# Storing rotated queries and keys to DRAM with the part as the outer index

## The chip, the core and the metric

The kernel runs on one core of a Trainium2 chip. A core has TensorE (PE, matmuls; PEld is its weight load), VectorE (DVE), ScalarE (ACT), GpSimd (POOL) and SyncE (SP, which here only issues DMAs), and 16 DMA engines that move data between DRAM and the on-chip memory of 128 partitions. ACT issues some DMAs too. The metric is the device time of one execution in microseconds (us), as the median of several runs.

## What is computed

Two layers of a diffusion transformer over 1024 latent tokens of width 1024, with 256 context tokens as a prefix for the keys. The first layer puts a short gated convolution beside a differential attention with 2-D rotary positions; the second mixes by Fourier transforms. Each is followed by a squared-ReLU MLP. What matters here is the attention:

```python
def diff_attend(q, k, v, lam):
    s = jnp.einsum('bqhcd,bkhcd->bhcqk', q, k).astype(jnp.float32) * (DIFF_QK_DIM ** -0.5)
    p = jax.nn.softmax(s, axis=-1)
    pd = (p[:, :, 0] - lam * p[:, :, 1]).astype(v.dtype)
    return jnp.einsum('bhqk,bkhd->bqhd', pd, v)
...
            p = u @ w_in[j]
            q = rope_2d(heads_qk(p[..., Q0:K0]), row, col)
            k = rope_2d(heads_qk(p[..., K0:V0]), row, col)
            v = heads_v(p[..., V0:])
```

There are 4 heads (h), each with two halves (c) of 64 channels for q and k. A rotation takes pairs of channels, 32 pairs for a half.

## The kernel before

All matmuls are in float32 by splitting: an operand is a high part rounded to the short format plus a low rest, and a product is three matmuls (`mm3`, lines 89 to 91; `split`, line 98, makes the high part on ACT and the low part on another engine). The stages around the change run in this order:

- **Values** (to about 105 us): the normalized tokens are transposed into `UH`, `UL` (latent) and `CH`, `CL` (context), and v is projected.
- **Queries and keys** (about 105 to 230 us; line 540 on). For two pairs of heads (`hp`) and for q, then k (`which`), there are two weight tiles: tile `iA` gives the first channel of each rotated pair and `iA + 1` the second. A weight tile has 128 columns: (2 heads x 2 halves) x 32 pairs. PE multiplies tile `iA` with each block of 512 tokens (and for k with the 256 context tokens), then tile `iA + 1`; after each block of the second, `rotate` (line 431) makes four **parts** `rp0` to `rp3` on DVE, POOL and ACT: the two rotated channels, each as high and low part. A part is 128 rows x 512 tokens; its row index is (head, half) g = 0..3 times pair r = 0..31. The parts have three buffers each, so a block must be in DRAM before the third block after it is written.
- `rotate` returns four stores (line 448; line 560 for the context, which isn't rotated). `store` (line 379, its DMA is line 382) issues them on SP two blocks later.
- **Weights** come through ACT's own DMA queue: `w_load` (line 235, DMA on line 238) loads tile i + 2 into one of two `wraw`, and `w_parts` splits the next tile into `wh` on ACT and `wl` on POOL. ACT works in order: while a DMA that it is to issue has to wait, what stands behind waits too.
- Beside this, `Ada` loads slices `wa` of the modulation weights on SP (line 164, biases on line 186), seven ahead, and DVE sums them up (`tick`, lines 172 and 174).
- **Convolution** (about 230 to 375 us; line 574 on): twelve more weight tiles, two blocks each, with DVE work between, and its own stores `Ad` on line 382.
- **Attention** (375 to 600 us): for each head and half, `load_set(n)` (line 504) reads from DRAM a set with `q`, `k0`, `k1` and `kx` on 128 partitions, arranged as parts x pairs: `k0` is both high parts of k twice, `k1` and `kx` both low parts twice (latent and context tokens), and `q` its high and low parts in an order that depends on the half. There are eight sets in three buffers. Sets 0 to 2 are loaded before their use; sets 3, 5 and 7 take the buffer of a half that just finished and belong to the head that starts. `S` (lines 634 to 638) multiplies q with k, `M` takes the maximum (641), `E` the exponential on ACT (646).

The order of PE, DVE, ACT, POOL and SP is written out by hand up to the end of the convolution; after it, a scheduler orders the instructions by the due times in a table. Each engine, and SP's DMA queue, works in that order. All DMAs of SP and ACT share eight completion semaphores in turn, and one is issued only when the DMA before it on the same semaphore has landed.

The DRAM copies are `Qd` and `Kd`, one tensor for two heads each:

```python
    Qd = [dram.tile([4, 4, 32, N], F32, name=f"Qd{i}") for i in range(2)]
    Kd = [dram.tile([4, 4, 32, NK], F32, name=f"Kd{i}") for i in range(2)]
```

Before, their indices are (g, part, pair, token). A store of one part takes all four g, at a distance of four parts, and the 32 rows of each: 4 x 32 rows. A load takes two neighbouring parts of one g: 64 rows of one stride.

Of the kernel before, what the change touches and what calls it, by code (L numbers as in the profile page):

```python
# [21 lines left out]
N = 1024  # L22
NC = 256
D = 1024
KT = 8
NK = N + NC
# [7 lines left out]
def raw(ap):  # L34
    return ap.bitcast(F32)


def body(tc, nc, I, O, dbg=None):
# [10 lines left out]
    def popen(name, **kw):  # L49
        p = tc.alloc_tile_pool(name=name, bufs=kw.pop("bufs", 1), **kw)  # L50
        pools[name] = p
        return p

    def pclose(*names):
        for n in names:
            pools.pop(n).release()
# [41 lines left out]
    def split(hi, lo, src, eng=None):  # L98
        a = nc.scalar.copy(hi, src)  # L99
        return a, (eng or nc.vector).tensor_tensor(out=lo, in0=src, in1=raw(hi), op=ALU.subtract)  # L100
# [134 lines left out]
    def w_load(i):  # L235
        if i < len(wsrc):
            wraws[i] = pW.tile([P, D], F32, name="wraw", tag="wraw")
            nc.scalar.dma_start(out=wraws[i], in_=wsrc[i])
# [10 lines left out]
    def rows():  # L249
        return p0.tile([P, D], F32, name="xt", tag="xt", bufs=11)  # L250
# [48 lines left out]
    with tc.manual_schedule(engines={mybir.EngineType.PE, mybir.EngineType.DVE, mybir.EngineType.Activation,  # L299
# [3 lines left out]
        for k in range(KT):  # L303
            t = ([WVL, WVH] + UH + UL)[k % 6].rearrange("p k n -> p (k n)")
            for i in range(2):
# [4 lines left out]
                for j in range(2):  # L310
                    ps, c = aps[2 * i + j], slice(j * 512, j * 512 + 512)
# [67 lines left out]
    def store(*keep):  # L379
        while len(stores) > len(keep):  # L380
            for o, i in stores.pop(0):
                nc.sync.dma_start(out=o, in_=i)
# [33 lines left out]
    Qd = [dram.tile([4, 4, 32, N], F32, name=f"Qd{i}") for i in range(2)]  # L416
    Kd = [dram.tile([4, 4, 32, NK], F32, name=f"Kd{i}") for i in range(2)]
    Ad = [dram.tile([KT, P, N], F32, name=f"Ad{i}") for i in range(2)]
    def next_weights(i):
        w_load(i + 2)  # L420
        if i:
            w_parts(i + 1)

    def proj(i, bH, bL, n, tag="mm"):
        ps = ps1.tile([P, 512], F32, name="pj", tag=tag)
        wh, wl = wtiles[i]
        for k in range(KT):
            mm3(ps[:, :n], wh[:, k, :], wl[:, k, :], bH[:, k, :], bL[:, k, :], k == 0, k == KT - 1)
        return ps

    def rotate(pR, ada, pA, pB, c, dst, scale):
        parts = [pR.tile([P, 512], F32R, name=f"rp{i}", tag=f"rp{i}", bufs=3) for i in range(4)]
        t = [pR.tile([P, 512], F32, name=f"rt{i}", tag=f"rt{i}") for i in range(4)]
        nc.vector.tensor_tensor(out=t[0], in0=pA, in1=cosT[:, c], op=ALU.mult)
        nc.vector.tensor_tensor(out=t[2], in0=pB, in1=sinT[:, c], op=ALU.mult)
        nc.vector.tensor_tensor(out=t[1], in0=pA, in1=sinT[:, c], op=ALU.mult)
        nc.vector.tensor_tensor(out=t[3], in0=pB, in1=cosT[:, c], op=ALU.mult)
        nc.gpsimd.tensor_tensor(out=t[0], in0=t[0], in1=t[2], op=ALU.subtract)
        nc.gpsimd.tensor_tensor(out=t[1], in0=t[1], in1=t[3], op=ALU.add)
        ada.tick()  # L440
        for i in range(2):
            if scale is None:
                split(parts[i], parts[2 + i], t[i])
            else:
                nc.scalar.mul(parts[i], t[i], scale)
                nc.vector.scalar_tensor_tensor(out=parts[2 + i], in0=t[i], scalar=scale, in1=raw(parts[i]),
                                               op0=ALU.mult, op1=ALU.subtract)
        return [(dst[:, i, :, c], raw(parts[i])) for i in range(4)]


    class Conv:
# [52 lines left out]
    def load_set(n):  # L504
        h, c = n // 2, 1 - n % 2
        p = pools["pHqR" if n % 3 == 2 else "pHqL"]
        t = {nm: p.tile([P, w], F32R, name=nm, tag=f"{nm}{n % 3}")
             for nm, w in (("q", N), ("k0", NK), ("k1", N), ("kx", NC))}
        rows = lambda ap: ap.rearrange("i r n -> (i r) n")
        g = (h % 2) * 2 + c  # L510
        q, k = Qd[h // 2][g], Kd[h // 2][g]
        for i in range(2):
            r = slice(i * 64, i * 64 + 64)
            j = (i + c) % 2 * 2
            nc.sync.dma_start(out=raw(t["q"][r]), in_=rows(q[j:j + 2]))
            nc.sync.dma_start(out=raw(t["k0"][r]), in_=rows(k[0:2]))
            nc.sync.dma_start(out=raw(t["k1"][r]), in_=rows(k[2:4, :, 0:N]))
            nc.sync.dma_start(out=raw(t["kx"][r]), in_=rows(k[2:4, :, N:NK]))
        hsets[h, c] = t

    def load_v(h):
        vv = []
        for i in range(2):
            t = pHv.tile([P, 10, P], F32R, name=f"vs{i}", tag=f"vs{i}")
            nc.sync.dma_start(out=raw(t), in_=Vd[i][:, :, h * P:(h + 1) * P])
            vv.append(t)
        heads.setdefault(h, {})["v"] = vv
# [4 lines left out]
    with tc.manual_schedule(engines={mybir.EngineType.PE, mybir.EngineType.DVE, mybir.EngineType.Activation,  # L532
                                     mybir.EngineType.Pool, mybir.EngineType.SP}):
        w_load(2)
        cosT = pR.tile([P, N], F32, name="cosT", bufs=1)
        sinT = pR.tile([P, N], F32, name="sinT", bufs=1)
        nc.sync.dma_start(out=cosT, in_=I["rope_cos"])
        nc.sync.dma_start(out=sinT, in_=I["rope_sin"])
        ada = Ada(pAda, ada0[:4])
        for hp in range(2):  # L540
            for which in range(2):
                iA = hp * 4 + which * 2
                if iA:
                    next_weights(iA)
                blks = [(UH[b], UL[b], 512) for b in range(2)] + [(CH, CL, NC)] * which
                psA = []
                for blk in blks:
                    psA.append(proj(iA, *blk))
                    ada.tick(2)
                next_weights(iA + 1)  # L550
                dst = (Kd if which else Qd)[hp]
                for b, blk in enumerate(blks):
                    pB = proj(iA + 1, *blk, "tr")
                    if b < 2:
                        st = rotate(pR, ada, psA[b], pB, slice(b * 512, b * 512 + 512), dst, None if which else 0.125)
                    else:
                        parts = [pR.tile([P, 512], F32R, name=f"rp{i}", tag=f"rp{i}", bufs=3) for i in range(4)]
                        split(parts[0][:, :NC], parts[2][:, :NC], psA[b][:, :NC])
                        split(parts[1][:, :NC], parts[3][:, :NC], pB[:, :NC])
                        st = [(dst[:, i, :, N:NK], raw(parts[i][:, :NC])) for i in range(4)]  # L560
                    stores.append(st)
                    store(0, 1)
                    ada.tick()
        ada.tick(len(ada0) * KT)
        ada.end()
        store()
        pclose("pAda", "pR", "pUc")
        pC = popen("pC", bufs=1, side="right", **tile_waits)
        cb = [pC.tile([P, 514], F32, name=f"cb{i}") for i in range(2)]
        for b in range(2):  # L570
            nc.gpsimd.memset(cb[b][:, 0:1], 0.0)
        ada = Ada(popen("pAda", side="right", **tile_waits), ada0[4:])
        pHv = None
        for c in range(12):
            i = 8 + c
            cv = Conv(c)
            next_weights(i)
            for b in range(2):
                cv.Y(b)
            for b in range(2):  # L580
                ps = proj(i, UH[b], UL[b], 512, ("mm", "tr")[b])
                ada.tick(2)
                cv.V(b, ps)
                cv.O(b)
                if not b:
                    store()
            if c == 7:
                ada.tick(len(ada0) * KT)
            if c == 8:
                ada.end()  # L590
                pclose("pAda")
                popen("pHqL", side="left", **tile_waits)
                pHv = popen("pHv", bufs=2, side="left", **tile_waits)
                load_set(0)
            if c == 9:
                load_v(0)
                load_set(1)
        store()
# [246 lines left out]
    tiles.update({i: Tile(i) for i in range(32)})  # L845
    last = {c: PIPE["S", c, 1] for c in range(2)}
    at(-1.0, lambda: load_set(2))
    for n in range(3, 8):
        m = n - 3
# [4 lines left out]
    for h in range(4):  # L854
        k = PIPE["SC",] + 4 * h + 3
# [1138 lines left out]
```

## Time and profile before

| | |
|---|---|
| median of 3 runs | 2353.55 us (2352.23 to 2354.19) |
| the profiled execution | 2347.32 us, its span 2345.2 us |
| PE busy | 2130.1 us, 91% of the span, 9618 matmuls |
| DVE, ACT, POOL busy | 63%, 36%, 51% |
| granted TensorE clock, mean | 0.965 of full speed |
| the chain that ended last, by engine | PE 50%, DVE 16%, POOL 9%, DMA 9%, issue 6%, ACT 5%, SP's queue 2% |

The profile is one execution, and its rows are in its own time. An engine's busy share is an average over stages that have different limits; the waits of one stretch say who was late there. "SPq" and "ACTq" are the DMA instructions of SP and ACT: their duration is the time in which the queue was held by issuing, not the transfer. A releaser is inferred from semaphores: the engine or DMA whose end came last before the wait was over.

### The profile page before, as it was taken

The page shows a single profiled execution, that of the slowest core. Times are in us where ns is not written, and L with a number is a line of the kernel's source. Part 1 is how long each engine was busy: PE and PEld are TensorE (multiplying, and loading weights), DVE is VectorE, ACT ScalarE, POOL GpSimd, SP SyncE. Part 2 cuts the span into 40 slices and gives each one's busy share as a digit, 9 for nine tenths or more (in the row PEclk, how much of TensorE's full clock was granted, in tenths as well). Part 3 has the DMA queues.
Part 4 walks back from the last instruction along what each step waited for, and adds up shares of the span by engine and source line. Part 5 has one row for each costly group of instructions (what it writes and reads, how often), then busy time and mean ns, then how long its engine had stood idle before and what let it go on. Part 6 is the DMA issues. An engine that isn't in the chain of part 4 may idle for free.

```text
span 2345.2 us, 26449 instructions
## 1 busy us (share of the span) xinstructions
PE 2130.1 (91%) x9618; PEld 1712.3 (73%) x9618; DVE 1487.9 (63%) x1893; ACT 832.7 (36%) x1254; POOL 1199.1 (51%) x767
## 2 busy tenths in 40 slices
PE   7997798888898999999999999897599998999986
PEld 3886686777776777777888887676477776778765
DVE  7464564898466775666434435537766664788888
ACT  5311113666344111221222224427444444533321
POOL 3433234778346333333458454738555553756596
PEclk9998898999999999999999999999799999999998
DMA  7454647453356333433223222433344335344333
GB/s 285 164 171 147 212 120 192 114 129 96 90 155 218 115 114 106 137 117 99 77 81 121 97 75 108 143 148 122 112 150 145 139 129 206 135 141 155 122 121 125
DMA packets 145329, 318.62 MB, mean 136 GB/s; under 512 B 17234, under 2 KB 47186, under 8 KB 144944
## 3 DMA queue, kind: packets, MB, share of 16 engines
q1 hardware_dynamic: 140128, 298.74, 38.5%
q10 hardware_dynamic: 4032, 12.58, 1.7%
q0 software_dynamic: 1040, 5.62, 0.7%
q8 instruction: 75, 1.23, 0.2%
q14 instruction: 54, 0.44, 0.1%
HBM read 241.90 MB, written 75.00 MB: 135 GB/s over the span
## 4 chain that ended last, share of the span: by engine, by line
PE 50%; DVE 16%; POOL 9%; DMA 9%; issue 6%; ACT 5%; SPq 2%; ACTq 0%; POOLq 0%; DVEq 0%
PE bky L89 8%; PE bky L91 7%; PE bky L90 7%; PE bkh L90 5%; PE bkh L91 5%; PE bkh L89 5%; DMA wa<-in_ada_w 3%; PE pj L91 2%; PE pj L89 2%; PE pj L90 2%; DVE s L1208 1%; DVE aacc L174 1%; DVE wl L100 1%; DMA hs<-Hs 1%; POOL ra L908 1%
## 5 line engine op out<-in xcount | busy, mean ns | idle before, releaser
L89 PE MATMUL bky<-wh,hh 128*128 128x512 f32 x728 | 283.7, 399 | 24.8 <-DVE acc L1045 12.0
L90 PE MATMUL bky<-wl,hh 128*128 128x512 f32 x728 | 287.9, 396 | 1.7 <-POOL wl L100 1.7
L1045 DVE TENSOR_TENSOR acc<-bky,acc 128x512 f32<-128x512 f32 x224 | 151.9, 688 | 145.3 <-PE bky L91 145.1
L91 PE MATMUL bky<-wh,hl 128*128 128x512 f32 x512 | 201.6, 394 | 0.0
L1029 POOL TENSOR_TENSOR hl<-r,hh 128x512 fp32r<-128x512 f32 x64 | 92.9, 1451 | 204.0 <-DVE r L1028 194.9
L89 PEld LDWEIGHTS bky<-wh,hh 128*128 128x128 f32 x728 | 138.1, 190 | 63.4 <-DVE acc L1045 17.4
L1295 POOL TENSOR_TENSOR hs<-hs,hh 128x1024 fp32r<-128x1024 f32 x48 | 130.9, 2735 | 93.9 <-ACT hh L1294 85.3
L992 ACT CAST wh<-wraw 128x1024 fp32r<-128x1024 f32 x64 | 65.7, 1050 | 317.5 <-PE bky L91 224.5
L90 PEld LDWEIGHTS bky<-wl,hh 128*128 128x128 f32 x728 | 138.6, 190 | 32.4 <-POOL wl L100 2.1
L174 DVE SCALAR_TENSOR_TENSOR aacc<-wa,cs,aacc 128x512 f32<-128x512 f32 x140 | 138.3, 988 | 36.8 <-DMA wa<-in_ada_w 34.5
L89 PE MATMUL pj<-UH,wh 128*128 128x512 f32 x320 | 129.6, 405 | 24.0 <-ACT wh L99 24.0
L993 POOL TENSOR_TENSOR wl<-wraw,wh 128x1024 fp32r<-128x1024 f32 x28 | 69.3, 2481 | 131.2 <-ACT wh L992 131.2
L100 POOL TENSOR_TENSOR w<-s,w 128x512 fp32r<-128x512 f32 x64 | 91.4, 1441 | 78.4 <-ACT w L99 77.4
L91 PE MATMUL pj<-UH,wl 128*128 128x512 f32 x320 | 126.6, 396 | 3.2 <-POOL wl L100 3.2
L90 PE MATMUL pj<-UL,wh 128*128 128x512 f32 x320 | 126.3, 395 | 0.0
L100 POOL TENSOR_TENSOR wl<-wraw,wh 128x1024 fp32r<-128x1024 f32 x21 | 51.3, 2444 | 142.6 <-ACT wh L99 73.2
L1028 DVE TENSOR_TENSOR r<-r 128x512 f32<-128x512 f32 x64 | 60.1, 944 | 87.3 <-ACT hh L1027 83.7
L91 PEld LDWEIGHTS bky<-wh,hl 128*128 128x128 f32 x512 | 97.0, 189 | 21.6
L89 PE MATMUL bky<-BH,w 128*128 128x512 f32 x256 | 101.8, 398 | 8.6 <-DVE t L1256 7.0
L991 POOL TENSOR_TENSOR wraw<-wraw,gateg 128x1024 f32<-128x1024 f32 x32 | 79.3, 2478 | 46.6 <-DMA wraw<-in_w 41.8
L90 PE MATMUL bkh<-UB,wh 128*128 128x512 f32 x256 | 101.5, 396 | 0.6 <-POOL UB L135 0.6
L89 PE MATMUL bkh<-UB,wh 128*128 128x512 f32 x256 | 101.4, 396 | 0.0
(517 smaller groups left out, 6219.4 us busy)
## 6 DMA issues: line engine op xcount, KB each, us to landing
wa<-in_ada_w SPq DMA_DIRECT2D x160, 256.0 KB
wraw<-in_w SPq DMA_DIRECT2D x66, 512.0 KB
hs<-Hs SPq DMA_DIRECT2D x48, 512.0 KB
Hs<-h SPq DMA_DIRECT2D x94, 256.0 KB
wr<-in_w SPq DMA_DIRECT2D x32, 512.0 KB
xt<-in_ada_w SPq DMA_DIRECT2D x16, 512.0 KB
xt<-in_x SPq DMA_DIRECT2D x16, 512.0 KB
e<-in_w SPq DMA_DIRECT2D x16, 512.0 KB
```

The lines of the kernel that those rows point to most:

```text
L89: nc.tensor.matmul(ps, aH, bH, start=start, stop=False, **kw)
L90: nc.tensor.matmul(ps, aH, bL, start=False, stop=False, **kw)
L91: nc.tensor.matmul(ps, aL, bH, start=False, stop=stop, **kw)
L100: return a, (eng or nc.vector).tensor_tensor(out=lo, in0=src, in1=raw(hi), op=ALU.subtract)
L174: nc.vector.scalar_tensor_tensor(out=acc[0], in0=wa, scalar=cs[:, k, 0:1], in1=acc[0], op0=ALU.mult, op1=ALU.add)
L991: nc.gpsimd.tensor_tensor(out=w, in0=w, in1=g, op=ALU.mult)
L992: nc.scalar.copy(wh, w)
L993: eng.tensor_tensor(out=wl, in0=w, in1=raw(wh), op=ALU.subtract)
L1028: nc.vector.tensor_tensor(out=r, in0=r, in1=r, op=ALU.mult)
L1029: pace[0] = nc.gpsimd.tensor_tensor(out=hl[:, c], in0=r, in1=raw(hh[:, c]), op=ALU.subtract)
L1045: pace[1] = nc.vector.tensor_tensor(out=a[:, c], in0=ps, in1=a[:, c], op=ALU.add)
L1295: nc.gpsimd.tensor_tensor(out=h, in0=raw(h), in1=raw(hh), op=ALU.subtract)
```

## The change

The letters of the DRAM index are exchanged: (part, g, pair, token) instead of (g, part, pair, token). The sizes of `Qd` and `Kd` stay, since both indices have four values. A store now covers 128 rows of one stride (`lanes` joins g and pair). For a load the two parts of one g no longer are neighbours, so each set is read in four pieces of 32 rows instead of two of 64, 16 DMAs instead of 8.

```diff
-        return [(dst[:, i, :, c], raw(parts[i])) for i in range(4)]
+        return [(lanes(dst[i])[:, c], raw(parts[i])) for i in range(4)]
+
+    def lanes(ap):
+        return ap.rearrange("g r n -> (g r) n")
...
-        rows = lambda ap: ap.rearrange("i r n -> (i r) n")
         g = (h % 2) * 2 + c
-        q, k = Qd[h // 2][g], Kd[h // 2][g]
-        for i in range(2):
-            r = slice(i * 64, i * 64 + 64)
-            j = (i + c) % 2 * 2
-            nc.sync.dma_start(out=raw(t["q"][r]), in_=rows(q[j:j + 2]))
-            nc.sync.dma_start(out=raw(t["k0"][r]), in_=rows(k[0:2]))
-            nc.sync.dma_start(out=raw(t["k1"][r]), in_=rows(k[2:4, :, 0:N]))
-            nc.sync.dma_start(out=raw(t["kx"][r]), in_=rows(k[2:4, :, N:NK]))
+        q, k = (d[h // 2][:, g] for d in (Qd, Kd))
+        for i in range(4):
+            r = slice(i * 32, i * 32 + 32)
+            a, j = i % 2, (i // 2 + c) % 2 * 2
+            nc.sync.dma_start(out=raw(t["q"][r]), in_=q[j + a])
+            nc.sync.dma_start(out=raw(t["k0"][r]), in_=k[a])
+            nc.sync.dma_start(out=raw(t["k1"][r]), in_=k[2 + a, :, 0:N])
+            nc.sync.dma_start(out=raw(t["kx"][r]), in_=k[2 + a, :, N:NK])
...
-                        st = [(dst[:, i, :, N:NK], raw(parts[i][:, :NC])) for i in range(4)]
+                        st = [(lanes(dst[i])[:, N:NK], raw(parts[i][:, :NC])) for i in range(4)]
```

On SP's queue the last stores of the keys stand, before, as follows (a name with its buffer number, written <- read, and the shape of the DRAM side; `wa_1857` is the first load for the convolution's `Ada`):

```order
L382 DMA Kd1_961<-rp3_1779 4x32x512
L382 DMA Kd1_961<-rp0_1820 4x32x256
L382 DMA Kd1_961<-rp1_1821 4x32x256
L382 DMA Kd1_961<-rp2_1822 4x32x256
L382 DMA Kd1_961<-rp3_1823 4x32x256
L382 DMA G2d0_955<-wa_1553 1x512
L164 DMA wa_1857<-in_ada_w 128x512
```

And now:

```order
L382 DMA Kd1_961<-rp3_1779 128x512
L382 DMA Kd1_961<-rp0_1820 128x256
L382 DMA Kd1_961<-rp1_1821 128x256
L382 DMA Kd1_961<-rp2_1822 128x256
L382 DMA Kd1_961<-rp3_1823 128x256
L382 DMA G2d0_955<-wa_1553 1x512
L164 DMA wa_1857<-in_ada_w 128x512
```

Nothing moved there; the shapes alone differ. In the load of set 2, at the start of attention, SP's queue before ends with the second of two pieces and goes on with the two loads of gates for the output stage:

```order
L515 DMA q_2853<-Qd0_958 64x1024
L516 DMA k0_2854<-Kd0_960 64x1280
L517 DMA k1_2855<-Kd0_960 64x1024
L518 DMA kx_2856<-Kd0_960 64x256
L865 DMA gateg1_2836<-in_ln_g 128x1024
L866 DMA gateg2_2837<-G1d_957 128x1024
```

And now with the fourth of four pieces:

```order
L517 DMA q_2869<-Qd0_958 32x1024
L518 DMA k0_2870<-Kd0_960 32x1280
L519 DMA k1_2871<-Kd0_960 32x1024
L520 DMA kx_2872<-Kd0_960 32x256
L867 DMA gateg1_2852<-in_ln_g 128x1024
L868 DMA gateg2_2853<-G1d_957 128x1024
```

The two gate loads stand behind eight more DMAs of SP than before. The other seven sets grow the same way in place. On PE, DVE, ACT and POOL the order is the same up to the output projection, after 597 us, where a few transposes, casts and matmuls change places within some 20 rows.

## Rows read from the trace of the kernel before

**Rows 1.** Waits of PE, 140 to 265 us: total us, times, longest us.

```profile
PE pj L89 <- ACT wh L99: 24.0, 2, 12.2
PE pj L91 <- POOL wl L100: 3.2, 3, 1.3
```

**Rows 2.** Chain of waits, 180 to 265 us: start us, us, what.

```profile
168.79 14.00 DMA Kd<-rp
...
251.84 6.02 DMA wa<-in_ada_w
```

**Rows 3.** Timeline of ACT, 186 to 262 us: start, us, instruction [idle before <-releaser].

```profile
189.53 0.63 ACT L445 ACTIVATE rp<-rt 128x512 fp32r<-128x512 f32 x1 [7.99 <-DMA Kd<-rp]
...
205.07 1.04 ACT L99 CAST wh<-wraw 128x1024 fp32r<-128x1024 f32 x1 [11.91 <-DMA wa<-in_ada_b]
...
258.30 1.04 ACT L99 CAST wh<-wraw 128x1024 fp32r<-128x1024 f32 x1 [21.31 <-DMA wa<-in_ada_w]
```

**Rows 4.** Line 382: count, duration ns min/median/max, first and last start us.

```profile
L382 SPq DMA_DIRECT2D Kd<-rp x24: 512/1806/3712, 162.4 to 247.1; - x24
...
L382 SPq DMA_DIRECT2D Ad<-coh x8: 319/332/650, 275.0 to 377.0; - x8
```

**Rows 5.** Stretches: length, busy us (x instructions) by engine, PE clock, DMA share, GB/s.

```profile
110.00:142.00 32.00, 32.00 (x152) 26.61 (x152) 22.21 (x28) 4.53 (x6) 10.96 (x6) 1.00 0.69 231
...
194.30:206.00 11.70, 0.00 (x0) 0.00 (x0) 6.26 (x10) 0.93 (x1) 0.00 (x0) 0.60 0.42 132
206.00:214.00 8.00, 6.57 (x15) 4.74 (x16) 0.65 (x2) 0.11 (x1) 2.35 (x1) 0.52 0.39 145
...
232.00:244.00 12.00, 12.00 (x55) 9.94 (x54) 0.00 (x0) 0.59 (x1) 1.17 (x1) 1.00 0.27 106
248.00:262.00 14.00, 1.34 (x3) 0.62 (x3) 4.47 (x4) 1.04 (x1) 2.35 (x1) 0.61 0.71 242
262.00:265.00 3.00, 3.00 (x8) 2.38 (x9) 2.93 (x5) 0.00 (x0) 0.00 (x0) 0.52 0.94 327
265.00:275.00 10.00, 10.00 (x44) 7.91 (x43) 9.75 (x16) 1.68 (x2) 2.41 (x1) 1.00 0.50 178
375.00:390.00 15.00, 6.63 (x26) 4.98 (x24) 6.97 (x8) 5.81 (x9) 5.49 (x3) 0.70 0.97 281
421.00:433.00 12.00, 9.44 (x65) 8.12 (x64) 10.84 (x14) 7.84 (x14) 7.40 (x4) 1.00 0.91 193
```

**Rows 6.** Timeline of SP, 138 to 262 us, equal neighbours merged.

```profile
221.10 28.32 SPq L382 DMA_DIRECT2D Kd<-rp  x12
...
251.41 8.43 SPq L164 DMA_DIRECT2D wa<-in_ada_w  x11
```

**Rows 7.** Timeline of SP, load of set 0.

```profile
341.27 0.52 SPq L515 DMA_DIRECT2D q<-Qd  x1
341.83 0.59 SPq L516 DMA_DIRECT2D k<-Kd  x1
...
343.10 0.59 SPq L518 DMA_DIRECT2D kx<-Kd  x1
...
345.66 0.65 SPq L518 DMA_DIRECT2D kx<-Kd  x1
```

**Rows 8.** Chain of waits, 420 to 434 us, load of set 3.

```profile
421.52 0.24 SPq L517
...
425.01 7.09 DMA k<-Kd
```

**Rows 9.** Timelines of SP, ACT and PE around the load of `gateg`.

```profile
381.25 0.58 SPq L865 DMA_DIRECT2D gateg<-in_ln_g  x1
...
387.63 1.06 ACT L1464 ACTIVATE gateg<-gateg 128x1024 f32<-128x1024 f32 x1 [6.67 <-DMA gateg<-in_ln_g]
...
390.04 0.80 PE L634 MATMUL s<-k,q 128*128 128x512 f32 x1 [6.54 <-ACT e L646]
```

**Rows 10.** Waits of PE in the output projection, 628 to 642 us, from its timeline.

```profile
631.14 0.78 PE L752 MATMUL bc<-ident,rbl 128*128 128x128 f32 x4 [2.47 <-ACT rbl L751]
```

## Prediction

> **What bounds the kernel now.** I began with the page: TensorE (PE) is busy for most of the span, so a change of DRAM layouts can only pay where PE stands still. The change touches the stage that projects queries and keys (about 105 to 262 us) and the loads of the attention stage (341 to 600 us), so I asked for PE's waits between 140 and 265 us. They come to two kinds: 24.0 us in two waits for ACT's `wh` and 3.2 us in three for POOL's `wl`, the two halves of one weight tile [rows 1]. PE stands from 194.3 to 206 us, works, and stands again for nearly all of 248 to 262 [rows 5]. The clock falls with it: granted 0.52 of 2.4 GHz (the lower level) from 206 to 214 and from 262 to 265 [rows 5].
>
> Who made ACT late? The chain of waits of that stretch runs through a store of `Kd` that took 14.00 us to land, then through the queue of SP, and at last through a load of `wa` of 6.02 us [rows 2]. ACT's own timeline says the same: one rotation waited 7.99 us for a `Kd` store, the tile that ends the first stall waited 11.91 us for `wa<-in_ada_b`, and the tile that ends the second 21.31 us for `wa<-in_ada_w` [rows 3]. ACT has no use for those two loads. It issues its own weight loads, and in this program a DMA is issued only when the earlier one that shares its semaphore has landed (eight serve all in turn); those two `wa` loads came earlier in that turn, and SP had issued them behind the stores. So SP being late makes ACT late.
>
> And why is SP late? The stores of `Kd` occupy SP for 1.81 us at the median, while a store of `Ad` at the same line, as large (128x512), takes 0.33 [rows 4]. Twelve `Kd` stores in a row hold SP for 28.32 us, 2.36 each; eleven `wa` loads, as large, take 8.43, 0.77 each [rows 6]. From 232 to 244 us, with nothing but such stores on the queue, the DMA engines are busy to 0.27 of their time and move 106 GB/s; from 262 to 265, with `wa` loads, 0.94 and 327 GB/s [rows 5]. So a store uses about a quarter of the DMA engines, for four times as long.
>
> *A rule beside this row.* The row shows a quarter in use and not why. The Trainium skill, "DMA: Bandwidth & Descriptors", section "Why a DMA increments its semaphore by 16 and not by 1", says that a DMA is spread over the largest number of engines, at most 16, that divides the slowest dimension of both its sides: 4 for 4x32x512 and 16 for 128x512. The trace agrees for the first (0.27 of the engines); of the 128-row form it has the 0.33 us of `Ad`. If it holds, the stores take a quarter of their time; if DRAM writes are slow for another reason, the second rival below is what comes.
>
> **The change, part by part.**
>
> *Stores.* The 40 stores of rotated parts keep their place, count and bytes; only their DRAM side becomes 128 rows of one stride. At 0.77 us of all DMA engines each (the `wa` row, the nearest of this size) instead of 2.36 of a quarter, twelve need 9.2 us and not 28.3. A piece with its four stores comes about every 5.5 us (24 matmuls of 0.227, from 265 to 275 us [rows 5]) and needs 3.1. SP then keeps up with the projections.
>
> What this gives back: PE's 24.0 + 3.2 = 27.2 us of waiting [rows 1], and the half clock after each stall: 15 + 3 + 8 = 26 matmuls took 6.57 + 1.34 + 3.00 = 10.9 us there [rows 5], against 26 x 0.227 = 5.9, so 5.0 more. Together **32.2 us**. What is late next? ACT's waits for the DMA ahead of the first stall are 7.99 + 11.91 = 19.9 us against 12 of PE standing; ahead of the second 21.3 against 12 [rows 1, 3]. About 8 and 9 us to spare remain in which a landing, the cast and POOL's half fit. I charge **1 us**; the bounds are 0 and one whole stall (13.5 us and its clock, about 16).
>
> That PE runs full beside a busy DMA is seen between 110 and 142 us, before the first store: no idle time at a DMA share of 0.69 [rows 5].
>
> *Loads.* Each of the eight sets for one head and half is now 16 loads instead of 8, with the same bytes: 64 more instructions on SP, all of them `q`, `k0`, `k1`, `kx`. Their order against everything else is kept; what stands behind a set moves back by eight issues. An issue of such a load takes (345.66 - 341.27) / 7 = 0.63 us [rows 7], with no difference between large and small ones, so eight more are **5.0 us** of SP. For a 32-row load the trace has no row; I take the 0.63 of the 64-row load, with 0.33 (`Ad` store) and 1.81 (`Kd` store) as the far ends [rows 4]. Where does it show?
> - Sets 0 and 1 are loaded beside the last convolution projections, and nothing on PE waits for them today; 10 us of SP are covered by the 34 us from the first load at 341 us to the stretch from 375 us on, in which attention starts [rows 5, 7]. Cost 0; if that cover were gone, at most 5.0.
> - Set 2 stands ahead of the load of `gateg`, for which ACT waits 6.67 us and PE then 6.54 [rows 9]. `gateg` would be issued 5.0 us later. But it lands 6.4 us after its issue (387.63 - 381.25) because the DMA engines are 0.97 busy there [rows 5], and the bytes ahead of it stay the same. Bounds 0 and 5.0; I take **1.5**, nearer to the row that says that the engines are the limit.
> - Sets 3, 5 and 7 reuse the buffers of the half just finished and are needed at once: loads are issued from 421.5 us on, and the last one PE needs is issued at 425.01 and lands 7.09 us later, when PE goes on [rows 8]. The engines are 0.91 busy there [rows 5]. With 16 issues the next to last comes 14 x 0.63 = 8.8 us after the first, at 430.3, and if it lands some 2.5 us later PE goes on at 432.8 and not at 432.1. Bounds 0 and 5.0 for each of three; I take 0.7, **2 us** in all. The loads of sets 4 and 6, of `vs` and of row sums behind them have most of a head to spare.
>
> *Order elsewhere.* On PE a few transposes and matmuls of the output projection swap places within some 20 rows; I take it as 0. The nearest row is a PE wait of 2.47 us there [rows 10]; 2.5 us either way bounds it.
>
> **Sum.** -32.2 + 1 + 1.5 + 2 = **-27.7 us**. The profiled execution would go from a span of 2345.2 to 2317.5 and from 2347.3 us to 2319.6. The median of the timed runs is 6.2 us above the profiled one; I keep that distance: 2353.55 - 27.7 = 2325.9, so **2326 us**.
>
> **Rivals.**
> 1. *One stall stays.* With the stores fast, ACT's weight loads still wait for SP's DMAs, and DVE and POOL still rotate; if the next latest of these is over 8 us late, one of the two stalls returns. Against it: the spare time above. One stall is 13.5 us and 2 to 3 of clock: -27.7 + 15 = -13, **2341 us**.
> 2. *The stores don't get faster.* If it is DRAM, and not the spreading over engines, that holds them, only the loads' 3.5 us are left: **2357 us**, within what a measurement of this kernel can tell from no change (0.2%, 4.7 us). Against it: 0.27 of the engines busy and 106 GB/s, where the same queue moves 327 GB/s [rows 5].
> 3. *The added loads cost more than the stores gave* (the other side). At four places (`gateg` and sets 3, 5, 7) PE waits for the end of a set. If an issue of a 32-row load takes x and nothing hides it, each place is later by 16x - 5.0. It decides from x = 0.8 us, where 4 x 7.8 = 31 eats the whole gain. At twice today's 0.63, 4 x 15.2 = 61 and the time is 2353.55 - 31.2 + 61 = **2383 us**. For it: `Kd` issues of 1.81 us do exist [rows 4]. Against it: those came with engines that were blocked, and `kx`, with a fifth of the bytes of `k0`, takes as long to issue [rows 7], so nothing shows an issue that grows as rows shrink. At x = 0.63 with nothing hidden the four cost 20, and the time is 2342: that is the top of my range.
>
> *A rule that speaks against the change.* The same page, section "Rules for kernel authors", asks to coalesce small transfers, since under 64 KB one pays mostly overhead, and to prefer one 128-partition transfer over pieces. `kx` falls to 32 KB by it. Were each of the 64 added loads to cost the page's fixed 2 us with nothing beside it, an estimate from that page is 128 us, the third rival and worse. The trace disagrees as far as it shows: a 64 KB `kx` today costs its 0.6 us of issue like the others.
>
> 4. *More than the sum.* The loads cost nothing and waits of DVE and SP that I left out shorten the start of the convolution: below 2318.
>
> **How the numbers follow.** Forecast (2318 to 2334) 0.60; one stall stays 0.17; more than the sum 0.10; stores not faster 0.06; loads dearer 0.07. Faster by over 0.2%: 0.60 + 0.17 + 0.10 = 0.87; within 0.2%: 0.06; slower: 0.07. The range goes from 2317 (32.2 in full, and 4 us of the distance between profiled run and median) to 2342 (one stall, or the loads fully exposed), and leaves out the two last cases and half of the larger gain.
>
> **What would show it right or wrong.** Right: `Kd` and `Qd` stores near 0.33 to 0.6 us each on SP; a DMA share well over 0.27 while they run; no wait of PE for `wh` between 140 and 265; PE at full clock through that stretch; the convolution starting about 30 us earlier. Each of the loads' terms is right if a set's sixteen issues take about 10 us, PE's wait ahead of the third tile (6.54 today) grows by no more than 2, and the first second-half scores of a head come no more than 1 us later after the set's first issue. Wrong: stores still over 1.5 us each (rival 2), a remaining wait of 10 us or more for `wh` (rival 1), or issues of over 0.8 us and PE waits for `k` at the head starts (rival 3).

## The result and the profile after

The changed kernel takes **2314.28 us** (median of 4 runs, 2313.40 to 2324.28) beside 2352.89 us for the kernel before (4 runs, 2350.94 to 2354.19): a ratio of 0.9841 with a 95% interval of 0.9818 to 0.9863. It is faster by 38.6 us. The forecast was 2326 us with a range of 2317 to 2342: the direction and the mechanism were right, the size was too small, and the time lies below the range.

The profiled execution took 2314.93 us. Its page, span and PE:

```profile
span 2313.2 us, 26522 instructions
PE 2129.0 (92%) x9618; PEld 1712.9 (74%) x9618; DVE 1491.9 (64%) x1893; ACT 831.9 (36%) x1254; POOL 1197.7 (52%) x767
```

The stage that was to gain. In four stretches of it (columns as in [rows 5]) PE is busy without a gap, where it had stood for nearly all of 194 to 206 and of 248 to 262:

```profile
142.00:166.00 24.00, 24.00 (x117) 20.01 (x116) 17.47 (x24) 5.03 (x8) 10.49 (x6) 1.00 0.79 261
166.00:190.00 24.00, 24.00 (x105) 19.52 (x104) 17.17 (x21) 4.52 (x6) 10.95 (x6) 1.00 0.78 261
190.00:212.00 22.00, 22.00 (x119) 18.84 (x118) 11.44 (x18) 5.02 (x8) 9.68 (x8) 1.00 0.30 107
212.00:230.00 18.00, 18.00 (x82) 14.88 (x80) 8.55 (x10) 2.61 (x4) 3.09 (x2) 1.00 0.97 349
```

The view of waits has no row for PE from 100 to 345 us, so both kinds of wait in [rows 1] are gone, and the granted clock is 1.00 throughout (0.52 after each stall before, [rows 5]). The stores show why. First the row of line 382 for `Kd` (duration in ns: min, median, max), then SP's timeline, which answers to [rows 4, 6]:

```profile
L382 SPq DMA_DIRECT2D Kd<-rp x24: 319/390/1054, 157.0 to 212.1; - x24
```

```profile
201.58 10.94 SPq L382 DMA_DIRECT2D Kd<-rp  x12
212.61 0.26 SPq L382 DMA_DIRECT2D G2d<-wa  x1
212.96 14.76 SPq L164 DMA_DIRECT2D wa<-in_ada_w  x16
```

A store holds SP for 0.39 us at the median (1.81 before), and the last twelve are out at 212.5 us, not at 249.4. The loads of `wa` follow at once. In the loads of the sets (answers to [rows 7]) an issue takes 0.42 us, not 0.59:

```profile
L518 SPq DMA_DIRECT2D k<-Kd x32: 302/419/468, 308.3 to 505.4; - x32
```

And around the gate row (answers to [rows 9]) ACT waits 7.97 us where it had waited 6.67, and PE behind it 8.90 where it had waited 6.54:

```profile
355.50 1.06 ACT L1466 ACTIVATE gateg<-gateg 128x1024 f32<-128x1024 f32 x1 [7.97 <-DMA gateg<-in_ln_g]
```

```profile
357.92 0.80 PE L636 MATMUL s<-k,q 128*128 128x512 f32 x1 [8.90 <-ACT e L648]
```

**Where the time went.** Matching each ACT instruction of the two traces gives the shift of the changed kernel against the one before; the last column is the step from the line above.

| place (time before) | shift, us | step |
|---|---|---|
| before the first store (to 160) | 0 | |
| convolution (300 to 380) | -33.4 | -33.4 |
| behind the gate row (from 380) | -32.1 | +1.3 |
| the heads (490 to 600) | -31.8 | +0.3 |
| output projection and after (740 to 800) | -28.6 | +3.2 |
| from 1420 | -32.2 | -3.6 |
| end | -32.0 | +0.2 |

In this pair of traces the gain, 33.4 us, stands in the stage that the change names, and the steps behind it add up to +1.4. The timed medians differ by 38.6 us, not by 32.0; the other 6.6 stand in no row of this table, and the first experiment and the account of the forecast come back to them.

### The profile page after: what moved, and what is told of

Read it like the earlier page. It is cut to its first block, busy times and chain, and to the rows that moved or that the text cites. A ratio compares the mean times of both kernels' runs of the same rounds, so it can differ in the third digit from the quotient of the medians.

```text
span 2313.2 us, 26522 instructions
## 1 busy us (share of the span) xinstructions
PE 2129.0 (92%) x9618; PEld 1712.9 (74%) x9618; DVE 1491.9 (64%) x1893; ACT 831.9 (36%) x1254; POOL 1197.7 (52%) x767
## 4 chain that ended last, share of the span: by engine, by line
PE 58%; DVE 16%; POOL 8%; ACT 5%; DMA 5%; issue 5%; SPq 0%; POOLq 0%; DVEq 0%; ACTq 0%
PE bky L89 8%; PE bky L90 8%; PE bky L91 8%; PE bkh L90 6%; PE bkh L91 5%; PE bkh L89 5%; PE pj L90 3%; PE pj L89 3%; PE pj L91 3%; DMA wa<-in_ada_w 2%; DVE s L1210 1%; DVE aacc L174 1%; POOL ra L910 1%; ACT xn L909 1%; DVE wl L100 1%
## 5 line engine op out<-in xcount | busy, mean ns | idle before, releaser
L90 PEld LDWEIGHTS bky<-wl,hh 128*128 128x128 f32 x728 | 138.7, 191 | 33.4 <-POOL wl L100 3.0
```

What stands on the lines that cost most here:

```text
L90: nc.tensor.matmul(ps, aH, bL, start=False, stop=False, **kw)
```

## Experiments

### The kernels again: how firm is a single time?

Before the causes, the yardstick. The forecast took the profiled execution of before (2347.32 us) and added its distance to the median. The kernel before, as it is:

> The kernel before, unchanged. Its first profiled execution took 2347.3 us, its timed runs 2351 to 2354; the prediction took those 6 us to be a fixed distance between profile and timing. Fixed distance: a second profile is again near 2347 and the timed runs are all near 2353. Scatter: the timed runs spread over 2347 to 2355, and the second profile lies elsewhere in it, with the difference in one or two late stretches (the 10.6 us load of bB near 1404 us is the first suspect).

Measured: 2352.57 us (median of 12, 2344.88 to 2361.16), ratio 1.0001 (0.9984 to 1.0019). The profiled one of these runs had a span of 2353.4 us, 8.2 longer than the first. Both pages' row of PE, the first profile and this one:

```profile
PE 2130.1 (91%) x9618; PEld 1712.3 (73%) x9618; DVE 1487.9 (63%) x1893; ACT 832.7 (36%) x1254; POOL 1199.1 (51%) x767
```

```profile
PE 2140.0 (91%) x9618; PEld 1719.6 (73%) x9618; DVE 1488.3 (63%) x1893; ACT 832.8 (35%) x1254; POOL 1195.9 (51%) x767
```

The same 9618 matmuls took 9.9 us longer (and their weight loads, PEld, 7.3); DVE, ACT and POOL agree within 4 us, and PE's idle time (span less busy) is 1.7 us shorter, not longer. The matching of instructions puts 8.3 us of the difference between 600 and 1100 us. The same stretch in both (columns: length, PE busy, granted clock, DMA share, GB/s):

```profile
600.00:1100.00 500.00, 472.40 (x2074) 0.98 0.40 130
```

```profile
600.00:1100.00 500.00, 472.73 (x2043) 0.96 0.39 127
```

So the granted clock differs from one execution to the next: 0.02 of 500 us is about 10 us of clock. The timed runs say the same. All 57 runs of the kernel before in these comparisons, by the mean clock that each records:

| mean granted clock | runs | median us | from, to |
|---|---|---|---|
| 0.958 to 0.960 | 16 | 2355.4 | 2350.6, 2362.3 |
| 0.961 to 0.963 | 22 | 2353.2 | 2344.7, 2358.1 |
| 0.964 and over | 19 | 2349.0 | 2340.6, 2355.6 |

The correlation is -0.67 (between -0.56 and -0.73 in each of the four sets of runs by itself), and 0.001 of clock goes with 1.2 us. The first profiled execution of before had 0.965 and belongs to the group with the lowest times. Its 6.2 us below the median were this scatter and not a distance that a profile keeps. A pair of single traces therefore carries some 8 us of scatter, and the 32.0 us of the table above has to be read with that. (That the clock is the cause is read from the two traces; the table alone is a correlation.)

The changed kernel again:

> The changed kernel, unchanged. Its first runs took 2313.4, 2313.6, 2314.9 (profiled) and 2324.3 us. Scatter theory: again 2312 to 2325, with a median near 2315 and a gain of 33 to 38 us. Fixed distance: timed runs 6 us above the profiled one.

Measured: 2314.79 us (median of 4, 2312.31 to 2316.64), ratio 0.9838 (0.9818 to 0.9858). The result stands.

### Is it the one stride? One unused row

The changed kernel with a gap behind each 32 rows of the DRAM copies, so that a store's 128 rows are four blocks again. Bytes, order in DRAM and loads are those of the changed kernel:

```
-    Kd = [dram.tile([4, 4, 32, NK], ...)]        # lanes: "g r n -> (g r) n"
+    Kd = [dram.tile([4, 4, 33, NK], ...)]        # lanes: ap[:, 0:32]
```

> The changed kernel with one unused row behind each 32 rows of the DRAM copies, so that a store again has 4 blocks of 32 rows and not one run of 128 rows of one stride; the loads stay those of the changed kernel (32 rows each). Theory (the store's cost follows from whether its 128 rows are one stride): all of the gain goes. A K store costs 2.3 to 2.4 us again, the stretch after the last matmul before the ag block has a DMA share near 0.27 as in the kernel before, PE waits 27 us (plus or minus 4) for wh and wl, and the time is that of the loads-alone kernel, 2349 us (2343 to 2358). Rival (it is the order of the blocks in DRAM, the part outermost, or the smaller loads that gain): the time stays at 2315 us (2311 to 2320) and PE has no wait between 105 and 262 us.

Measured: 2348.66 us (median of 10, 2344.11 to 2355.50), ratio 0.9992 (0.9977 to 1.0007). No gain is left that these runs can tell from zero. PE's waits from 105 to 265 us, then the stretch of [rows 5] with nothing but stores on the queue:

```profile
PE pj L89 <- ACT wh L99: 23.6, 2, 12.1
PE pj L91 <- POOL wl L100: 3.1, 3, 1.3
```

```profile
232.00:244.00 12.00, 12.00 (x55) 9.93 (x54) 0.00 (x0) 0.59 (x1) 0.81 (x1) 1.00 0.27 104
```

Both stalls are back at their old size, and the share of 0.27 with them. That the part is the outer index, or that loads are smaller, gains by itself at most the 5.4 us that the interval leaves; the 34 us between this run and the changed kernel (medians 2348.7 and 2314.6) come from a store being one run of 128 rows of one stride.

With one unused row behind each 64 rows (`[4, 2, 65, NK]`) a store has two blocks:

> As the kernel with one unused row behind each 32, but one behind each 64 rows: a store has 2 blocks of 64 rows. Theory (the number of engines that a store uses follows its outermost count): DMA share near 0.13 while only stores run, twice the price, 4.7 us for 256 KB, and 40 stores of this kind set the stage: the K and Q stores take some 50 us more than the stage has room for, so 2400 us (2370 to 2430). Rival (a store is slow whenever its rows are not one stride, however many blocks there are): 2.4 us for 256 KB and 2349 us (2340 to 2358).

Measured: 2439.36 us in one run, 9 us above the range expected. A stretch without matmuls, and the last twelve stores:

```profile
310.00:330.00 20.00, 0.00 (x0) 0.00 (x0) 0.00 (x0) 0.00 (x0) 0.00 (x0) 0.52 0.13 51
```

```profile
283.06 53.59 SPq L382 DMA_DIRECT2D Kd<-rp  x12
```

Two blocks: 0.13 of the engines and 51 GB/s. Four blocks: 0.27 and 104. The twelve stores take 53.59 us, 28.32 [rows 6] and 10.94 with two blocks, four blocks and one run. The shares are those of two and of four engines out of 16, at about 26 GB/s each: in this case's runs, the number of blocks on the DRAM side gives the engines in use. This is the rule of the Trainium skill, "DMA: Bandwidth & Descriptors", section "Rules for kernel authors", that an outermost dimension below 16 confines a DMA to at most that many engines; both steps of the trace agree with it.

### Do the added loads cost anything?

The layout and the stores of before, but each set loaded by 16 DMAs of 32 rows:

```
-        for i in range(2):      # 64 rows, source rows(k[0:2])
+        for i in range(4):      # 32 rows, source k[i % 2]
```

> Layout and stores of the kernel before, but each set read in four pieces of 32 rows (16 loads). From the comparison of the two profiles: +1.3 us at gateg, +0.3 at the heads, +3.2 where the output projection is ordered otherwise, so a loss near 5 us against the kernel before (2357). From the prediction's terms: +3.5. Rival that loads are dear: +20 or more.

Measured: 2348.66 us (median of 10, 2345.59 to 2357.18), ratio 0.9991 (0.9976 to 1.0006). No cost that can be measured, and the 2357 of the expectation and the 3.5 us of the forecast did not come: the interval ends at 1.4 us above the kernel before. The kernel with one unused row behind each 32, which has the same loads, the same order on PE and slow stores as well, has the same median; together these 20 runs are 4.2 us below the 57 of the kernel before by medians (2348.66 and 2352.82), though neither run by itself can be told from no change. The loads' own terms are seen one by one in the trace against that of before: the ACT instructions shift from -0.4 to +1.0 us at the gate row (1.4; the forecast said 1.5) and by another 0.6 at the three sets loaded late (the forecast said 2). PE's longest wait behind the gate row is 9.0 us here:

```profile
PE s L634 <- ACT e L646: 15.0, 8, 9.0
...
PE s L634 <- DMA k<-Kd: 0.3, 1, 0.3
```

A 32-row issue is cheaper than one of 64 rows (0.42 us against 0.59), so 16 issues, where nothing holds them, follow each other in 7.4 us and not in the 10 us that the forecast assumed. The Trainium skill, same page and section, warns that transfers under 64 KB are mostly overhead; the runs here, with 64 more loads, and 32 pieces of `kx` at 32 KB each, show none in the time.

The other way round: the layout and stores of the changed kernel, with the loads of 64 rows that the code of before had, which are now two blocks of 32:

```
-        for i in range(4):      # 32 rows: q[j + a], k[a], ...
+        for i in range(2):      # 2 x 32 rows: q[j:j + 2], k[0:2], ...
```

> The changed kernel (its layout, its stores), but each set of heads is loaded by 8 DMAs of 2 blocks of 32 rows instead of 16 DMAs of 32 rows. Theory (the engines that a transfer uses follow its outermost count, for loads too): the 128 KB load, which takes 2.3 to 6.7 us from issue to landing now, takes the price of 2 engines, 2.4 us for 128 KB behind each other, so a set of some 900 KB takes about 16 us where its sixteen loads are issued in 7.4 us now; the first sets and the gate loads come late, PE waits for k and q 10 to 25 us in sum, and the time is 2330 us (2320 to 2345). Rival (loads from DRAM are not bound to the outermost count, or the sets come early enough): within 4 us of the changed kernel, 2311 to 2319 us.

Measured: 2510.87 us (median of 4, 2507.88 to 2516.09), ratio 1.067 (1.0649 to 1.0691). The direction was expected, the size missed by far. PE's waits from 300 to 900 us, and a stretch in which it does nothing:

```profile
PE s L636 <- DMA k<-Kd: 85.9, 3, 34.3
PE s L636 <- ACT e L648: 49.2, 9, 44.4
PE s L636 <- DMA vs<-Vd: 35.6, 1, 35.6
PE s L637 <- DMA k<-Kd: 21.9, 5, 5.3
```

```profile
360.00:380.00 20.00, 0.00 (x0) 0.00 (x0) 0.00 (x0) 0.00 (x0) 0.00 (x0) 0.50 0.13 52
```

The price per byte was right (0.13 of the engines, 52 GB/s). Two other things were wrong. The expectation put a set at some 900 KB; its 128 rows of 1024 + 1280 + 1024 + 256 floats make 1.8 MB, 35 us at this rate. And it paid for one set, while SP's queue is in order, so that the sets, the loads of `vs` and of the gate row behind them are late one after the other: the four waits come to 193 us. So the 64 added loads are no side effect of the change but what makes it possible: this layout with loads of 64 rows is some 160 us slower than the kernel before.

### Is it SP's time, or the time until a store lands?

The layout of before, each store cut into four of 32 rows of one stride:

```
-        return [(dst[:, i, :, c], raw(parts[i])) for i in range(4)]
+        return [(dst[g, i, :, c], raw(parts[i][g * 32:g * 32 + 32])) for i in range(4) for g in range(4)]
```

> Layout and loads of the kernel before (8 per set), but each part is stored by four DMAs of 32 rows instead of one of 4 x 32 (160 stores instead of 40). If the outer count of 4 held the stores to a quarter of the DMA engines: PE's waits for wh between 140 and 265 us vanish as with the change, a gain of 33 us in that stage and none given back by loads, about 2313 to 2316. If the distance of four parts between the rows (the layout) is what made them slow: no gain, about 2352. If 160 issues of some 0.45 us are too many for SP: a part of the 33, with stores late.

Measured: 2334.03 us (median of 4, 2330.91 to 2337.18), ratio 0.9921 (0.9899 to 0.9942): about half of the gain. PE's waits from 105 to 265 us, the stretch that held the first stall before, and SP's last batch:

```profile
PE ag L193 <- DVE aacc L174: 6.9, 1, 6.9
PE pj L91 <- POOL wl L100: 1.3, 1, 1.3
```

```profile
190.00:212.00 22.00, 22.00 (x119) 18.77 (x118) 12.48 (x19) 5.13 (x8) 9.61 (x8) 1.00 0.65 177
```

```profile
210.65 25.76 SPq L382 DMA_DIRECT2D Kd<-rp  x48
```

The parts lie in DRAM as they did before, so their distance there is not what made the stores slow. The five batches of `Kd` and `Qd` stores hold SP for 16.43 + 12.06 + 17.12 + 16.32 + 25.76 = 87.7 us here and for 83.3 before (33.1 after the change), and yet both waits for `wh` are gone. The stores land fast here: by stretch, a part's pieces land 1.7 to 4.7 us after their issue at the median. Of the stores of before the profile gives no such median, only the one of 14.00 in the chain [rows 2].

Does this refute "SP being late makes ACT late"? It does not, because four times as many stores also take other turns at the eight semaphores. Before, the two weight loads that ended the stalls waited for `wa<-in_ada_b` and `wa<-in_ada_w`, which SP issued behind stores. Here are the same two loads of ACT, then SP's issues of those DMAs:

```profile
184.20 0.34 ACTq L238 DMA_DIRECT2D wraw<-in_w_cv  x1
...
219.84 0.36 ACTq L238 DMA_DIRECT2D wraw<-in_w_cv  x1
220.24 1.05 ACT L99 CAST wh<-wraw 128x1024 fp32r<-128x1024 f32 x1 [1.42 <-DMA Kd<-rp]
```

```profile
192.65 0.35 SPq L186 DMA_DIRECT2D wa<-in_ada_b  x1
...
236.83 15.62 SPq L164 DMA_DIRECT2D wa<-in_ada_w  x17
```

ACT's loads leave 8.5 and 17.0 us before SP issues what they had waited for. So SP can hold its queue as long as before without a stall when the stores land fast and ACT's turn falls on other DMAs; which of the two freed ACT, this run does not tell apart, and it leaves the link of the prediction neither confirmed nor refuted. In the changed kernel, where the order of the queues is that of before in this stretch, the second of these loads leaves 6.0 us after SP has begun with its `wa` loads (212.96), which is what the link says:

```profile
218.93 0.34 ACTq L238 DMA_DIRECT2D wraw<-in_w_cv  x1
```

What SP's own time costs here is the new wait: the `wa` loads are still issued behind the stores, DVE sums them late, and PE waits 6.9 us for the sum. With 1.3 us for `wl` and some 3 us at half clock behind it, that is about 11 of the 12 us by which this stage falls short of the changed kernel's. By the medians the run is 19.4 us above the changed kernel (2334.0 and 2314.6); the 7 us outside this stage are not explained.

### Can the next wait be taken away?

The longest wait of PE that is left in this part is 8.9 us behind the gate row. Its loads put ahead of set 2:

```
-    at(0.5, lambda: nc.sync.dma_start(out=gate["g1"], ...))     # and g2
+    at(-1.1, lambda: nc.sync.dma_start(out=gate["g1"], ...))
```

> The changed kernel, with the two loads of the gate rows put ahead of the loads of head set 2 in SP's queue. In the changed kernel ACT waits 7.97 us for gateg and PE 8.9 us for ACT behind it, with 10.2 us of half clock after it. Theory (the gate rows wait only because 16 loads of a set stand ahead of them on SP): PE's wait goes and with it half of the half-clock stretch, 9 to 13 us; 2304 us (2301 to 2308). Rival (the gate rows' own data, or the set that is now behind them, is as late): 2314 us (2311 to 2318), with a new wait of PE for k of set 2.

Measured: 2316.51 us (median of 4, 2308.77 to 2320.53), ratio 0.9838 (0.9813 to 0.9862): no change against the changed kernel. The 2304 of the expectation did not come; the time is the rival's, without the wait for `k` that the rival named. The timeline of ACT:

```profile
347.47 1.06 ACT L1466 ACTIVATE gateg<-gateg 128x1024 f32<-128x1024 f32 x1 [3.19 <-DMA gateg<-in_ln_g]
```

PE's wait fell from 8.9 to 4.8 us only: the load was issued at 342.5 us only, after SP had waited 2.2 us for it (by the profile for a matmul of PE's projections, line 91), and ACT got it 5 us later. Then also the scaling of the gate row moved from ACT to POOL:

```
-    nc.scalar.mul(gB, gB, ALPHA)
+    nc.gpsimd.tensor_scalar(gB, gB, ALPHA, 0.0, ALU.mult, ALU.add)
```

> The kernel with the gate loads first, and the scaling of the gate row (the only early user of those loads) done by POOL instead of ACT. In the kernel with the gate loads first alone ACT still waited 3.19 us for gateg and PE 4.8 us behind it, and the half-clock stretch behind that wait was as long as before, 10.2 us. Theory (what holds PE at the start of attention is ACT's place in line behind the gate row): the 4.8 us wait goes, down to the 1 to 2 us that PE waits there for DVE's maximum and ACT's exponential, the half-clock stretch at 349 goes with it, and the time is 2305 us (2301 to 2310). Rival (POOL's own first softmax step is now late behind the gate row, and PE waits for it instead, or the time is lost again in the scatter of the half-clock stretches further on): 2314 us (2311 to 2318).

Measured: 2310.84 us (median of 5, 2307.45 to 2314.78), ratio 0.9822 (0.9807 to 0.9837). POOL takes the row without holding anyone, and PE's longest wait for ACT in attention is 1.9 us:

```profile
345.53 1.05 POOL L1466 TENSOR_SCALAR gateg<-gateg 128x1024 f32<-128x1024 f32 x1 [0.64 <-DMA gateg<-in_ln_g]
```

```profile
PE s L636 <- ACT e L648: 7.9, 8, 1.9
```

The wait went as expected, but the time is 0.8 us above the range of the expectation and just below its rival. The instructions behind the wait come 5.5 us earlier; in this profiled execution (2314.4 us, near the slowest of the five) 5 of the 5.5 us are lost again further on. By medians it is 3.8 us below the eight runs of the changed kernel (2314.6), with overlapping intervals: a step in the right direction, not one that these runs prove.

## Why the forecast fell short

The gain was forecast at 27.7 us and measured at 38.6 by medians. The mechanism held. What failed is a term of the sum: the added loads, with the order elsewhere put at 0, were charged 3.5 us, and the runs show no such cost: by medians, kernels with these loads are 4.2 us below the kernel before. The stores' term was 2 to 3 us too small as well.

**What bounds the kernel: right.** The stall, its place and the reason (a quarter of the engines) hold: one unused row brings the stalls back. The link by which SP's lateness holds ACT was read from the rows of before; the changed kernel agrees with it, and no run takes it away by itself.

**Stores: right in kind, a little short in size.** Forecast 32.2 less 1 of residue, 31.2; measured 33.4 in the traces, and 34.0 between the medians of the changed kernel (8 runs) and of the two kernels with the same loads and slow stores (20 runs). The PE waits gave their 27.2 us in full. The half clock behind them was estimated at 5.0 and no residue came; some 1 us of the 33.4 I can't assign.

**Loads and the order elsewhere: the step that failed.** Charged +3.5 us: 1.5 for the gate row, 2 for the three late sets, 0 for the order. In the traces the gate row cost 1.3 us (1.4 with the loads alone) and the three late sets 0.3 (0.6 with the loads alone) where 2 was charged, since the 32-row issue was taken at 0.63 us apart, the spacing for 64 rows, and is 0.465. In the timed runs the two kernels that have these loads, this order and slow stores end their intervals at +1.4 and +1.6 us and have a median 4.2 us below that of the kernel before. By medians that is 7.7 of the 10.9 us by which the gain was forecast short; 2.8 are the stores, and the rest is in which runs of the two kernels are taken together. By the intervals alone, about 2 us of it are sure. Where a gain of some 4 us would come from is open: up to 600 us the traces of these kernels show only the small losses above, and past it a single trace scatters by more. The third rival, dearer loads, has no support left. One sign that the forecast set itself failed: PE's wait ahead of the third tile was to grow by no more than 2 us and grew by 2.4 (6.54 to 8.90), though the instructions behind it moved by 1.3 only.

**Order in the output projection: put at 0, not settled.** The +3.2 us there and the -3.6 at 1420 us look like costs and gains of the reorder, but the kernel before against itself shifts by 8.3 us in the same part, with the clock. No run isolates the reorder. If the 4 us are its doing, the bound of 2.5 us either way was too narrow; that is not shown.

**The distance to the median: misread, but not the error.** The forecast took 6.2 us for a distance that a profile keeps, and it was the scatter of one execution: after the change the profiled execution ran 0.65 us slower than the median. Yet adding the distance back is the same as taking the gain off the median of the timed runs, and that median held (2353.55; 2352.82 in 57 runs). Without it the forecast would have been 2319.6 and nearer, by luck: the fast execution of before hides about 6 us of the gain, so that the two profiled executions differ by 32.4 us and the medians by 38.6. The low end of the range, which let go of 4 of the 6.2 us with the stores at 32.2 and no more, left no room for loads that cost less than nothing.

**Rivals.** One stall stays: no, PE has no wait there. Stores not faster: no, with the padded kernels as proof of the cause. More than the sum, given 0.10, is what came, for half of its reason: the loads cost nothing that can be measured, but the waits of DVE and SP at the start of the convolution that it named are not what the traces show. The rule on engines beside [rows 5] held for two blocks, for four and for a run of 128.

## What to carry to other kernels

When a store or load is slow and the DMA engines are mostly idle, look at the side in DRAM: count the blocks that do not merge into one stride, and lay the tensor out so that all 128 rows do. Give the same look to whoever reads the tensor: a layout that is good for the store can leave its loads in two blocks, and more, smaller transfers of one stride beat fewer in blocks. A single profiled execution is a sample: two of one kernel differed by 8 us here, and the pair of traces showed 32 us of a gain that the medians put at 38.6. Take the yardstick from the timed runs, and check each term of a sum on a kernel that has that part of the change alone.

## What was unexpected

- A 32-row load of the same row length holds the queue for less time than a 64-row one (0.42 us against 0.59), and a 128-row store for 0.39 at the median.
- The engines in use followed the blocks closely: 51 to 52 GB/s for two, for stores and loads alike, 104 for four.
- Two kernels with twice the loads and slow stores ran no slower than the kernel before; by medians they were 4 us faster, and why is open.
- Executions of one program differ by up to 22 us (2340.6 to 2362.3 in 57 runs), with the granted clock: in the two traces of before, matmul time differs by 9.9 us where the spans differ by 8.2.
